# Side loads of x, first weights and gate combinations put behind other work in the instruction streams of a two-layer decoder kernel

## The chip, the core and the metric

The kernel runs on one core of one Trainium2 chip. The metric is the device time of one execution in microseconds; of the kernel before there are three timed runs and one profiled execution. The core has five engines with an instruction stream of their own: PE (TensorE, the matmuls), DVE (VectorE), ACT (ScalarE), POOL (GpSimd) and SP (SyncE), which here does nothing but issue DMA transfers. Each of the last four does its stream strictly in order, so an instruction that waits holds up everything behind it on that engine.

## The reference

The input x is 2048 tokens x 1024 features in float32. One chunked gMLP layer (layer A) is followed by one layer of dilated attention (layer B) that reads a shared key/value projection. Cut to what matters here:

```python
h = rms_norm(x, norm_g) * (1 + scale) + shift          # layer A
u, v, z = split(h @ w_in, 3)                           # 1024 -> 3 x 2048
v = rms_norm(gelu(v), sgu_g)
mixed = einsum('gts,bcsge->bctge', tril(w_s), chunks(v)) + b_s
x = x + gate * ((gelu(u) * mixed * silu(z)) @ w_out)   # 2048 -> 1024
k, v = split(ada(rms_norm(x)) @ w_kv, 2)               # shared, 6 kv heads of 128
q, z = ada(rms_norm(x)) @ w_in_b                       # 24 query heads, and 1024 of z
o = softmax-merge of three dilated attention groups
x = x + gate * ((o * silu(z)) @ w_out_b)
```

All projections are matrix products of 512 tokens with weight blocks; they fill most of the time of PE.

## The kernel before, in words

**Tiles and stages.** The tokens are taken in four quarters Q = 0 to 3 of 512 tokens (four tiles of 128). Quarter 0 runs layer A, then its share of layer B's projections (kv, q, z). Quarters 1 and 2 run layer A together in `layer_half`: first the v blocks (`dense_v`, names vh4 and vh5), then eight groups of u and z (`gate_block`, names uh0 to uh7 and zh0 to zh7), then each its output product and projections. Quarter 3 is like quarter 0, with its v blocks done by `dense_s2` (names v3). Attention for what is ready is woven in between as "fillers": Python generators that are advanced a step at a time by `tick` after every few matmuls.

**Precision.** Every product takes three matmul passes (`mm3`, L301): each operand is split into a high part and a low remainder, and high x high, low x high and high x low are summed. A weight block therefore takes this path: SP loads it raw (`raw_...`, 256 KB, L280, six buffers), ACT copies it to the high part (L272, about 0.63 us), DVE subtracts to get the low part (L273, about 0.69 us), and PE uses both (`w_...`, eight buffers). A weight unit that is late at any of the three is a stall of PE.

**Products.** Most blocks are done by Strassen-Winograd's 2x2 scheme with seven products. A product's name in a weight's name tells its weight block: 11, 12, 21, 22 are blocks as they are, t1 to t4 are combinations; `w_vh4t2_0` is the first unit of the t2 product of vh4. In the gates the combinations are made on the way, by DVE subtractions of loaded blocks (L744, `less`), since their tiles are small (128x512).

**Side work that the change touches.** `normed_T` prepares a later quarter's normalised and transposed input: it loads four tiles of x rows (`xa...`, 512 KB each, L864), squares them on ACT with a sum (L872), loads the transposed x (`xT...`, four pieces of 512 KB, L874), and makes the scale factors and products from both. It runs as a filler for quarter 1 (`xa00` to `xa03`, `xT1`), quarter 2 (`xa10` to `xa13`, `xT2`) and quarter 3 (`xa30` to `xa33`, `xT3`). `sums_A` loads quarter 3's stored input (`m3_1`) and makes sums of its parts (DVE, L1051 to L1054) and a split (`sA30`) that `dense_s2` uses from its fifth product on. `make_ops` makes split operands of layer B's input (`hob...`, L984 and L985). `product_out` adds the output product of layer A to the rows of x (`xr`, L1322), squares the sum on ACT (L1323), stores it (`x1d`, L1328), scales the rows (L1338), and PE transposes them (`pt_b`, L965, in `norm_T2`); in quarter 0 these transposes stand in the midst of the last output block's matmuls. `v_put` ends a v block's part with a gelu and a square on ACT (L1372, L1373), the latter over the PSUM tile itself.

**What sets the order.** The Tile framework's scheduler orders each engine's stream by its own cost model. `tc.issue_after(ins)` forces what is issued inside it to stand behind `ins`; it adds no wait across engines where the two are on one engine.

## Time and profile before

| | us |
|---|---|
| median of the three timed runs | 2913.62 |
| their lowest and highest | 2909.56, 2916.78 |
| time of the profiled execution | 2904.79 |
| span of its instructions | 2902.7 |
| PE busy in it | 2845.0 (98%) |
| DVE, ACT, POOL busy | 2199.5 (76%), 1629.5 (56%), 838.8 (29%) |
| DMA moved in it | 725.04 MB, mean 250 GB/s |
| mean granted clock of PE | 0.996 |

A busy PE here includes matmuls whose ends are modelled, so its 98% does not say that all of its time is at full speed. The time in which it stood still is told by the view of waits, and the time in which its clock was cut by the column PEclk of a view of time windows. The profile's lines carry the line numbers of the kernel; groups of tiles leave buffer numbers out, so `w_kv` stands for every weight unit of every kv block.

### The profile page before, as it was taken

The page shows a single profiled execution, that of the slowest core. Times are in us where ns is not written, and L with a number is a line of the kernel's source. Part 1 is how long each engine was busy: PE and PEld are TensorE (multiplying, and loading weights), DVE is VectorE, ACT ScalarE, POOL GpSimd, SP SyncE. Part 2 cuts the span into 40 slices and gives each one's busy share as a digit, 9 for nine tenths or more (in the row PEclk, how much of TensorE's full clock was granted, in tenths as well). Part 3 has the DMA queues.
Part 4 walks back from the last instruction along what each step waited for, and adds up shares of the span by engine and source line. Part 5 has one row for each costly group of instructions (what it writes and reads, how often), then busy time and mean ns, then how long its engine had stood idle before and what let it go on. Part 6 is the DMA issues. An engine that isn't in the chain of part 4 may idle for free.

```text
span 2902.7 us, 45106 instructions
## 1 busy us (share of the span) xinstructions
PE 2845.0 (98%) x14378; PEld 2381.9 (82%) x14378; DVE 2199.5 (76%) x4104; ACT 1629.5 (56%) x3302; POOL 838.8 (29%) x1097
## 2 busy tenths in 40 slices
PE   8999999999999999999999999999999999999999
PEld 5888878887888888878888788788888888888887
DVE  6877558787697789967787768789779676788682
ACT  4324346566556666545564656667666357876441
POOL 1067423440031025003315135115335121122322
PEclk9999999999999999999999999999999999999999
DMA  9899866888874655797989788855447867789653
GB/s 320 293 335 340 294 230 194 294 290 279 295 274 161 202 170 183 246 325 238 306 285 312 257 295 278 297 170 172 152 128 260 314 217 231 238 276 336 221 173 110
DMA packets 390449, 725.04 MB, mean 250 GB/s; under 512 B 42202, under 2 KB 119228, under 8 KB 389828
## 3 DMA queue, kind: packets, MB, share of 16 engines
q1 hardware_dynamic: 390212, 722.16, 74.3%
q8 instruction: 114, 1.87, 0.3%
q14 instruction: 123, 1.01, 0.1%
HBM read 547.81 MB, written 174.20 MB: 249 GB/s over the span
## 4 chain that ended last, share of the span: by engine, by line
PE 78%; DMA 8%; DVE 6%; issue 3%; ACT 3%; POOL 2%; SPq 0%; POOLq 0%; DVEq 0%; ACTq 0%
PE pd_kv L301 7%; PE po L1809 4%; PE pd_o L301 2%; PE pd_u L343 2%; PE pd_u L345 2%; PE pd_u L344 2%; PE pd_z L345 2%; PE pd_z L344 2%; PE pd_z L343 2%; PE pd_v L301 2%; PE pd_v3a L301 1%; PE pd_v3b L301 1%; PE pd_o3a L301 1%; PE pf L2002 1%; PE pf L2000 1%
## 5 line engine op out<-in xcount | busy, mean ns | idle before, releaser
L301 PE MATMUL pd_kv<-w_kv,hkh 128*128 128x512 f32 x672 | 209.3, 393 | 2.9 <-DVE w_kv L273 2.1
L1809 PEld LDWEIGHTS po<-kv,pT 128*128 128x128 f32 x1200 | 147.1, 191 | 15.7 <-POOL pT L1784 4.6
L1809 PE MATMUL po<-kv,pT 128*128 128x128 f32 x1200 | 150.6, 275 | 6.8 <-ACT pT L1655 2.8
L301 PEld LDWEIGHTS pd_kv<-w_kv,hkh 128*128 128x128 f32 x672 | 126.0, 189 | 30.7 <-DVE w_kv L273 3.2
L301 PE MATMUL pd_kv<-w_kv,hkl 128*128 128x512 f32 x336 | 131.0, 390 | 0.0
L272 ACT ACTIVATE w_q<-raw_q 128x512 fp32r<-128x512 f32 x144 | 89.1, 628 | 56.2 <-PE pd_kv L301 8.7
L1572 POOL TENSOR_SCALAR s_q<-s_q 128x4 f32<-128x4 f32 x96 | 24.2, 252 | 330.0 <-DVE s_q L1571 270.5
L1749 ACT ACTIVATE pr<-pr,stat,rt 128x256 f32<-128x256 f32 (+1 forms) x192 | 104.2, 545 | 25.8 <-DVE stat L1743 17.4
L1428 POOL TENSOR_SCALAR vc<-vc,rvh 128x256 f32<-128x256 f32 x64 | 65.4, 1041 | 183.7 <-DMA vc<-vh 132.5
L273 DVE TENSOR_TENSOR w_q<-raw_q,w_q 128x512 fp32r<-128x512 f32 x144 | 95.6, 685 | 22.2 <-ACT w_q L272 21.6
L2000 PE MATMUL pf<-wo,yb 128*128 128x512 f32 x256 | 104.5, 408 | 0.2 <-ACT yb L1963 0.2
L343 PE MATMUL pd_u<-hAh,w_u 128*128 128x512 f32 x256 | 103.5, 404 | 0.0
L343 PE MATMUL pd_z<-hAh,w_z 128*128 128x512 f32 x256 | 102.8, 401 | 0.0
L2002 PE MATMUL pf<-wo,yb 128*128 128x512 f32 x256 | 100.7, 394 | 0.0
L345 PE MATMUL pd_z<-hAh,w_z 128*128 128x512 f32 x256 | 100.3, 392 | 0.0
L345 PE MATMUL pd_u<-hAh,w_u 128*128 128x512 f32 x256 | 100.2, 391 | 0.0
L2001 PE MATMUL pf<-wo,yb 128*128 128x512 f32 x256 | 100.1, 391 | 0.0
L344 PE MATMUL pd_z<-hAl,w_z 128*128 128x512 f32 x256 | 99.9, 390 | 0.0
L344 PE MATMUL pd_u<-hAl,w_u 128*128 128x512 f32 x256 | 99.9, 390 | 0.0
L1749 ACT ACTIVATE st_pr<-st_pr,stat,rt 128x256 f32<-128x256 f32 (+1 forms) x128 | 73.5, 576 | 31.6 <-DVE stat L1746 18.2
L1757 POOL TENSOR_TENSOR dg<-pr,ident 128x256 f32<-128x256 f32 x38 | 31.2, 822 | 198.0 <-ACT pr L1749 132.6
L272 ACT ACTIVATE w_z<-raw_z 128x512 fp32r<-128x512 f32 x64 | 39.8, 628 | 81.8 <-PE pd_z L345 37.2
(1471 smaller groups left out, 8984.0 us busy)
## 6 DMA issues: line engine op xcount, KB each, us to landing
raw_q<-in_b_w_in_dram SPq DMA_DIRECT2D x144, 256.0 KB, 3.5
qt<-qd SPq DMA_DIRECT2D x96, 260.0 KB, 2.7
od<-ot SPq DMA_DIRECT2D x96, 256.0 KB, 3.0
w_o<-wtd SPq DMA_DIRECT2D x48, 512.0 KB, 5.2
raw_kv<-in_w_kv_dram SPq DMA_DIRECT2D x84, 256.0 KB, 4.1
kv<-kvd SPq DMA_DIRECT2D x75, 256.0 KB, 3.9
raw_u<-in_a_w_in_dram SPq DMA_DIRECT2D x64, 256.0 KB, 4.9
wt<-st_cw SPq DMA_DIRECT2D x64, 256.0 KB, 4.8
```

Source lines behind the costliest of these rows:

```text
L272: nc.scalar.activation(hi, src, AF.Copy)
L273: nc.vector.tensor_tensor(lo, src, hi.bitcast(F32), ALU.subtract)
L301: last_mm[0] = nc.tensor.matmul(pt, a, u[:, w, :], start=f, stop=e, skip_group_check=more)
L343: nc.tensor.matmul(pts[i], wh, hh[:, k, :], start=k == 0, stop=False)
L344: nc.tensor.matmul(pts[i], wh, hl[:, k, :], start=False, stop=False)
L345: nc.tensor.matmul(pts[i], wl, hh[:, k, :], start=False, stop=k == KT - 1)
L1428: nc.gpsimd.tensor_scalar(v[:, c, :], v[:, c, :], rvh[:, i:i + 1], None, ALU.mult)
L1749: nc.scalar.activation(pr[:, i, :], pr[:, i, :], AF.Exp, bias=mneg[:, i:i + 1], scale=u["rt"][:, h:h + 1], accum_out=lsum[:, i:i + 1])
L1809: nc.tensor.matmul(po[:, h * P:(h + 1) * P], u["pT"][h // hp][:, h % hp, j, :], u["kv"][:, j, kh, 1, :], start=j == 0, stop=j == nk - 1)
L2000: nc.tensor.matmul(pt, yb[:, 0, k, :], w_[:, 0, :], start=k == 0, stop=False)
L2001: nc.tensor.matmul(pt, yb[:, 0, k, :], w_[:, 1, :], start=False, stop=False)
L2002: nc.tensor.matmul(pt, yb[:, 1, k, :], w_[:, 0, :], start=False, stop=k == KT - 1)
```

## The change

Six edits of order; no instruction's work changes, and the only instructions that are added are three loads of activation tables on ACT, 93 in place of 90, that the new order brings with it.

1. `normed_T`: the loads of x rows and of xT are issued behind the last load of weights that the program has written so far (`last_ld`), and the squares behind the last high split of weights (`last_split[0]`).
2. `dense_v`: the splits of the product after "12/21" (the t2 product's) are issued behind the last square of the first half of that product's results.
3. `dense_o`: in its last product, the first weights of the kv projection are asked for ahead of the second half's matmuls.
4. `dense_s2`: the sums and the first split of `sums_A` are issued behind the low split of the t4 product's last weights.
5. `gate_block`: loading and combining a gate block's weights becomes a function of its own, `gate_raw`, called for the next block in the last product (t4) of the one before.
6. `make_ops`: the first puts ("11", "12") are issued behind the last splits of weights on ACT and DVE.

```diff
+    last_split = [None, None]
     def split(hi, lo, src):
-        nc.scalar.activation(hi, src, AF.Copy)
-        nc.vector.tensor_tensor(lo, src, hi.bitcast(F32), ALU.subtract)
+        last_split[0] = nc.scalar.activation(hi, src, AF.Copy)
+        last_split[1] = nc.vector.tensor_tensor(lo, src, hi.bitcast(F32), ALU.subtract)
...
-    def wunits(w, k0, n0, nm, nk=KT, ordered=False):
+    def wunits(w, k0, n0, nm, nk=KT, ordered=False, after=None):
...
-            split(u[:, 0, :], u[:, 1, :], raw)
+            with tc.issue_after(after.ins) if after else nullcontext():
+                split(u[:, 0, :], u[:, 1, :], raw)
...
                 if h:
                     store_late(0)
+                    if then is after:
+                        nxt.append(then())
...
-            nxt.append(then())
+            if then is not after:
+                nxt.append(then())
...
         ready = weights(b0, "t4")
-        late[0]()
+        with tc.issue_after(last_split[1].ins):
+            late[0]()
...
-    def gate_block(g, kind, ops, put, hooks={}):
+    def gate_raw(g, kind):
...
         raw["t3"] = raw["12"]
         less("t3", "22", "12")
+        return raw
+
+    def gate_block(g, kind, ops, put, raw, after, hooks={}):
...
             if w == "21":
                 raw["t4"] = raw["21"]
                 less("t4", "21", "t2")
+            if w == "t4":
+                raw.clear()
+                after()
             store_late(1)
...
         def c11(t, pt):
-            put(t, 0, pt, evt(f"{nm}a{t}"), pt)
+            return put(t, 0, pt, evt(f"{nm}a{t}"), pt)
...
+        half = []
         for a, q, first, take in (("11", "11", True, copy), ("12", "21", False, c11), ("s2", "t2", True, add_u),
...
-            us = wunits(*src[q], f"{nm}{q}_", 4)
+            us = wunits(*src[q], f"{nm}{q}_", 4, after=half.pop() if half else None)
...
                 for i in range(2):
-                    take(2 * pr + i, pts[i])
+                    done = take(2 * pr + i, pts[i])
+                if done and not pr:
+                    half.append(done)
...
             xts[t] = tile_of(t)
-            nc.sync.dma_start(xts[t], x[(Q * TPQ + t) * P:(Q * TPQ + t + 1) * P, :])
+            with tc.issue_after(last_ld[0].ins):
+                nc.sync.dma_start(xts[t], x[(Q * TPQ + t) * P:(Q * TPQ + t + 1) * P, :])
...
-            nc.scalar.activation(xts[t], xts[t], AF.Square, accum_out=sq[:, t:t + 1])
-        for k in range(0, KT, 2):
-            nc.sync.dma_start(xT[:, k:k + 2, :], x_t[k * P:(k + 2) * P, Q * QT:(Q + 1) * QT]
-                              .rearrange("(k p) t -> p k t", p=P))
+            with tc.issue_after(last_split[0].ins):
+                nc.scalar.activation(xts[t], xts[t], AF.Square, accum_out=sq[:, t:t + 1])
+        with tc.issue_after(last_ld[0].ins):
+            for k in range(0, KT, 2):
+                nc.sync.dma_start(xT[:, k:k + 2, :], x_t[k * P:(k + 2) * P, Q * QT:(Q + 1) * QT]
+                                  .rearrange("(k p) t -> p k t", p=P))
...
-            put("11", js, r0)
-            put("12", js, r1)
+            with tc.issue_after(last_split[0].ins), tc.issue_after(last_split[1].ins):
+                put("11", js, r0)
+                put("12", js, r1)
...
+        raws = {0: gate_raw(0, 0)}
         for g in range(8):
...
+            def prepare(i):
+                if i < 16:
+                    raws[i] = gate_raw(*divmod(i, 2))
+
-            gate_block(g, 0, ops, put_u)
-            gate_block(g, 1, ops, put_z, begin_y(got) if g == 7 else {})
+            gate_block(g, 0, ops, put_u, raws.pop(2 * g), lambda: prepare(2 * g + 1))
+            gate_block(g, 1, ops, put_z, raws.pop(2 * g + 1), lambda: prepare(2 * g + 2),
+                       begin_y(got) if g == 7 else {})
```

How this moves instructions is told by the streams themselves, at three places. The first is ACT at the end of quarter 0's output product. `w_o01_1_*` are the last output weights, `xa1*` rows of quarter 2's x, `w_kv02_*` the first weights of the kv projection, `xo0_1_*` the squares of the output rows on which the transposes `pt_b` depend. Before:

```order
L272 ACTIVATE w_o01_1_7_3472<-raw_o01_1_7_3473 128x512
L872 ACTIVATE xa11_4147,sqa2_4132<-xa11_4147 128x1024
L872 ACTIVATE xa12_4156,sqa2_4132<-xa12_4156 128x1024
L872 ACTIVATE xa13_4195,sqa2_4132<-xa13_4195 128x1024
L272 ACTIVATE w_kv02_0_0_3671<-raw_kv02_0_0_3672 128x512
L1323 ACTIVATE xo0_1_0_3531,sq10_0_2861<-xr0_0_2853 128x512
L1323 ACTIVATE xo0_1_1_3541,sq10_1_2862<-xr0_1_2854 128x512
```

After the change:

```order
L274 ACTIVATE w_o01_1_7_3472<-raw_o01_1_7_3473 128x512
L274 ACTIVATE w_kv02_0_0_3671<-raw_kv02_0_0_3672 128x512
L1349 ACTIVATE xo0_1_0_3531,sq10_0_2861<-xr0_0_2853 128x512
L1349 ACTIVATE xo0_1_1_3541,sq10_1_2862<-xr0_1_2854 128x512
L274 ACTIVATE w_kv02_0_1_3676<-raw_kv02_0_1_3677 128x512
```

The three squares of x rows are gone from here; they stand among the weights of the later block q02, and their loads and those of `xa00` with them have left SP's stream ahead of the store of the output rows. Likewise `xa00` to `xa03` move from block q02 to block q01, `xa30` to `xa33` from the kv blocks of quarter 2 to block q21, `xT2` from the start of the program to block q02, `xT1` and `xT3` behind the t4 loads of q01 and q21.

The second place is ACT at the turn from the product 12/21 to the product t2 of vh4. `pd_vh4a*` are PSUM tiles that the t2 product writes next; `ops*` are splits of another side work's sums (`fh*`). Before:

```order
L272 ACTIVATE ops3_6008<-fh511_6211 128x512
L272 ACTIVATE w_vh4t2_0_6236<-raw_vh4t2_0_6237 128x512
L272 ACTIVATE w_vh4t2_1_6241<-raw_vh4t2_1_6242 128x512
L272 ACTIVATE w_vh4t2_2_6246<-raw_vh4t2_2_6247 128x512
L1372 ACT_TABLE_LOAD
L1372 ACTIVATE vh4a0_6187<-pd_vh4a0_6022 128x512
L1372 ACTIVATE vh4a1_6190<-pd_vh4a1_6023 128x512
L1373 ACTIVATE pd_vh4a0_6022,sqh0_6010<-vh4a0_6187 128x512
L1373 ACTIVATE pd_vh4a1_6023,sqh0_6010<-vh4a1_6190 128x512
L272 ACTIVATE w_vh4t2_3_6251<-raw_vh4t2_3_6252 128x512
```

After the change:

```order
L274 ACTIVATE ops3_6008<-fh511_6211 128x512
L274 ACTIVATE ops4_6007<-fh512_6214 128x512
L1398 ACT_TABLE_LOAD
L1398 ACTIVATE vh4a0_6187<-pd_vh4a0_6022 128x512
L1398 ACTIVATE vh4a1_6190<-pd_vh4a1_6023 128x512
L1399 ACTIVATE pd_vh4a0_6022,sqh0_6010<-vh4a0_6187 128x512
L1399 ACTIVATE pd_vh4a1_6023,sqh0_6010<-vh4a1_6190 128x512
L274 ACTIVATE w_vh4t2_0_6236<-raw_vh4t2_0_6237 128x512
L274 ACTIVATE w_vh4t2_1_6241<-raw_vh4t2_1_6242 128x512
```

The t2 weights' high splits now stand behind the squares, and a split of another operand (`ops4` from `fh512`) stands ahead of the gelu. On DVE the low splits of `w_vh4t2_*` move in the same way behind three operations on `fh611` and `fh612`.

The third place is ACT at the start of gate block uh6, where attention's softmax (`stat1`, `kT0_3`) is woven in. `uh6t2` is a combination that DVE makes. Before:

```order
L1448 ACT_TABLE_LOAD
L1448 ACTIVATE pd_zh5t_9888<-pd_zh5t_9888 128x512
L774 ACTIVATE st_uh6u_10250<-pd_uh6x_10213 128x512
L1770 ACT_TABLE_LOAD
L1770 ACTIVATE stat1_195<-stat1_195 128x4
L1691 ACTIVATE kT0_3_10353<-pk0_3_10348 128x512
L1770 ACTIVATE stat1_195<-stat1_195 128x4
L272 ACTIVATE w_uh6t2_10253<-uh6t2_10209 128x512
L272 ACTIVATE w_uh6t1_10286<-uh6t1_10208 128x512
```

After the change:

```order
L1782 ACT_TABLE_LOAD
L1782 ACTIVATE pr0_2_01_10125,stat0_194<-pr0_2_01_10125,stat0_194,rt0_2_0_10016 128x256 x2
L1476 ACT_TABLE_LOAD
L1476 ACTIVATE pd_zh5t_9888<-pd_zh5t_9888 128x512
L793 ACTIVATE st_uh6u_10250<-pd_uh6x_10213 128x512
L274 ACTIVATE w_uh6t2_10253<-uh6t2_10160 128x512
L274 ACTIVATE w_uh6t1_10286<-uh6t1_10159 128x512
L274 ACTIVATE w_uh621_10339<-raw_uh621_10157 128x512
L1724 ACTIVATE kT0_3_10353<-pk0_3_10348 128x512
```

The split of the t2 combination stands directly behind the copy of the first product, the table load and the softmax pieces behind it; one more change of table stands shortly ahead.

More of the change, by code (lines that the diff above doesn't have):

```diff
@@ L1 @@
-from contextlib import ExitStack
+from contextlib import ExitStack, nullcontext
 from itertools import chain
@@ L749, in gate_block, with less @@
         less("t3", "22", "12")
+        return raw
+    def gate_block(g, kind, ops, put, raw, after, hooks={}):
+        nm = f"{'uz'[kind]}h{g}"
+        def less(o, a, b):
+            nc.vector.tensor_tensor(raw[o], raw[a], raw[b], ALU.subtract)
         def product(pt, a, w, first):
@@ L1372, in v_put @@
         nc.scalar.activation(dst, src, AF.Gelu_apprx_tanh)
-        nc.scalar.activation(junk, dst, AF.Square, accum_out=sqh[t // 4][:, t % 4, j:j + 1])
+        last = nc.scalar.activation(junk, dst, AF.Square, accum_out=sqh[t // 4][:, t % 4, j:j + 1])
         stores.append([0, lambda: nc.sync.dma_start(vh[t * P:(t + 1) * P, j * 512:(j + 1) * 512], dst)])
+        return last
     def in_long():
```

## The prediction

> **What bounds the kernel now.** The page gives PE 2845.0 of 2902.7 us, so I read first the waits of PE, to see which of its stops the six edits touch. Columns: engine, line, what it waited for, total us, times, longest.
>
> ```profile
> PE pt_b L965 <- DVE xr L1338: 5.1, 1, 5.1
> PE pd_vh4a L301 <- ACT pd_vh4a L1373: 4.3, 2, 3.6
> PE pd_uh6y L762 <- ACT w_uh6t L272: 2.7, 1, 2.7
> PE pd_v3a L301 <- ACT w_v L272: 2.3, 1, 2.3
> PE pd_kv L301 <- DVE w_kv L273: 2.1, 2, 1.1
> PE pd_zh3y L762 <- ACT w_zh3t L272: 1.7, 1, 1.7
> PE pd_v3a L301 <- DVE w_v L273: 0.9, 1, 0.9
> PE pd_zh5y L762 <- ACT w_zh5t L272: 0.9, 1, 0.9
> PE pd_uh6y L762 <- DVE w_uh6t L273: 0.3, 1, 0.3
> ```
>
> Together 20.3 us, at places where something that the edits move stands ahead of what PE needs. Second I read windows behind the long ones (stretch, its length, PE busy (matmuls), granted clock, DMA share, GB/s).
>
> ```profile
> 406.00:412.70 6.70, 4.88 (x15) 0.50 0.76 273
> 665.30:668.70 3.40, 3.40 (x10) 0.50 0.91 269
> 1102.20:1105.60 3.40, 3.08 (x8) 0.50 0.00 0
> 1849.70:1853.10 3.40, 3.40 (x10) 0.51 0.97 350
> ```
>
> After each of the four longest stops PE runs at half clock for a while. What it does there would take half the time at full clock, so the cuts cost 4.88/2 = 2.4, then 1.7, 1.5 and 1.7 us more. The most that the edits could win is 20.3 + 7.3 = 27.6 us, 1% of the span.
>
> **A rule on the clock.** [...] The rows show it halved after stops of 2.7 + 0.3 and of 2.3 + 0.9 us too. [...]
>
> **Quarter 0's output product (edit 1).** PE waits for the scaled rows of the output. What they wait for stands in the timelines (start, us, operation, idle before it and what ended it).
>
> ```profile
> 395.32 1.06 ACT L872 ACTIVATE xa<-xa 128x1024 f32<-128x1024 f32 x1 [3.70 <-DMA xa<-in_x_dram]
> 400.02 1.06 ACT L872 ACTIVATE xa<-xa 128x1024 f32<-128x1024 f32 x1 [3.54 <-DMA xa<-in_x_dram]
> 401.60 0.62 ACT L1323 ACTIVATE xo<-xr 128x512 f32<-128x512 f32 x1
> 396.52 1.29 DVE L1322 TENSOR_TENSOR xr<-xr,xo 128x512 f32<-128x512 f32 x2
> 406.92 0.76 DVE L1338 TENSOR_SCALAR xr<-xr,r_b 128x1024 f32<-128x1024 f32 x1 [2.16 <-DMA x1d<-xr]
> 396.50 5.02 SPq L864 DMA_DIRECT2D xa<-in_x_dram  x2
> 401.62 0.86 SPq L1328 DMA_DIRECT2D x1d<-xr  x2
> 407.82 1.09 PE L965 MATMUL pt_b<-ident,xr 128*128 128x128 f32 x4 [5.14 <-DVE xr L1338]
> ```
>
> The two row tiles are summed by 397.2 and 397.8, but their squares begin at 401.6, behind squares of x rows that wait 3.7 and 3.5 us for their loads. The store is late as well: SP sits from 396.50 on loads of x rows whose buffers those squares free, and issues it at 401.62. The scaling, which overwrites the rows, waits for the store until 406.92. With the x rows off both engines, squares and store begin at about 397.8, 3.8 us earlier. From 401.62 to 406.92 took 5.3 us, so the scaling comes at 403.1 and PE at 404.0 in place of 407.8. Its stop is then 5.1 − 3.8 = 1.3, shorter than any that was followed by a cut: 5.1 + 2.4 − 1.3 = 6.2. If the store no longer holds the scaling up (2.16), the stop is gone: 7.5. If the transposes, which now stand up to 8 matmuls earlier in PE's stream, give that shift back as a wait (8 x 0.23 = 1.8), it is 4.4. I take **+6.2**, range 4 to 7.5.
>
> **vh4 (edit 2).** PE waits here for the squares of the first half's results. Taken by itself the edit promises the whole stop, 3.6 + 1.7.
>
> ```profile
> 658.02 0.69 DVE L926 TENSOR_TENSOR fh<-fh 128x512 f32<-128x512 f32 x1
> 661.63 1.28 ACT L1372 ACT_TABLE_LOAD   x1
> 662.92 1.08 ACT L1372 ACTIVATE vh4a<-pd_vh4a 128x512 f32<-128x512 f32 x2
> 665.06 0.69 DVE L926 TENSOR_TENSOR fh<-fh,fh 128x512 f32<-128x512 f32 x1
> 664.67 7.36 PE L301 MATMUL pd_vh4a<-w_vh4t,ops 128*128 128x512 f32 x24 [3.57 <-ACT pd_vh4a L1373]
> ```
>
> But in the new stream the split of `fh512` stands ahead of the table load. DVE's first operation on it is the row of 658.02; with the low split of `fh511` and the second operation, 0.7 us each, it is ready at about 660.0. Its high split ends at 660.6, the table load at 661.9, one us earlier than now, the squares at about 664.0, and the first t2 weight's high split, now behind them, at 664.6: PE could start when it does now. The low split of that weight stands on DVE behind the row of 665.06 and ends at 666.4, while PE asks for it two matmuls in, at 665.1. That is 1.3 us lost. Behind it on DVE wait the three other low splits, 0.7 each, faster than PE uses them. I take **−1.3**. The bounds are +5.3, if the loads of `fh` come early enough to clear both engines, and −2.6, if another operation of 1.3 gets in. vh5's t2 splits are treated alike: table load 1.3, gelu 1.1, squares 1.2, first split 0.7 + 0.7 make 5.0 us from the end of a half product, and the other half keeps PE busy for 24 matmuls, 7.36 − 1.7 = 5.7 at full clock: 0, and a stop of under 1 if one more operation gets in.
>
> **Gates (edit 5).** The start of uh6:
>
> ```profile
> 1097.36 1.28 ACT L1770 ACT_TABLE_LOAD   x1
> 1098.30 1.09 DVE L744 TENSOR_TENSOR uh6t<-raw_uh,raw_uh 128x512 f32<-128x512 f32 x1 [0.66 <-DMA raw_uh<-in_w_uz_dram]
> 1100.41 1.15 ACT L272 ACTIVATE w_uh6t<-uh6t 128x512 fp32r<-128x512 f32 x2 [0.97 <-DVE uh6t L744]
> ```
>
> ACT splits at 1100.41 because DVE combined from 1098.3 to 1100.3, and that because the load had just landed. Begun a product earlier (12 matmuls, 2.7 us, and the attention pieces between) the combination is there in time. The stops of uh6 (2.7 + 0.3 and 1.5 of clock), zh3 (1.7) and zh5 (0.9) make 7.1. Against it stand three table loads more, 3 x 1.28 = 3.8 us of ACT. With none of them on PE's path the gain is 7.1, with all of them 3.3; I take the middle, **+5.2**, since some stand ahead of a gelu whose PSUM tile PE writes next and some do not. The range goes down to 0, if such a gelu comes late twice.
>
> [...]
>
> **kv weights (edits 3 and 6).** The kv stops are low splits that stand behind four low puts of `hob`:
>
> ```profile
> 1277.30 2.49 DVE L985 TENSOR_TENSOR hob<-st_b,hob 128x512 fp32r<-128x512 f32 x4
> 1280.31 0.68 DVE L273 TENSOR_TENSOR w_kv<-raw_kv,w_kv 128x512 fp32r<-128x512 f32 x1
> ```
>
> The puts go behind kv weights, and nothing reads them before the q products that follow the kv blocks. 2.49 is more than the longest stop, 1.1. **+2.0**, range 1 to 2.1. Edit 3 leaves SP's stream here as it was: 0.
>
> **v3 (edit 4).**
>
> ```profile
> 1843.24 1.23 DVE L1053 TENSOR_TENSOR m<-m 128x1024 f32<-128x1024 f32 x1
> 1846.50 2.17 ACT L272 ACTIVATE w_v<-raw_v 128x512 fp32r<-128x512 f32 x4
> 1838.67 2.35 SPq L280 DMA_DIRECT2D raw_v<-in_a_w_in_dram  x4
> raw_v<-in_a_w_in_dram SPq DMA_DIRECT2D x48, 256.0 KB, 4.2
> 1843.78 1.07 PE L301 MATMUL pd_z2bb<-w_z2b,hob 128*128 128x512 f32 x4
> ```
>
> The first weight lands at 1838.7 + 4.2 = 1842.9. With no sums and no `sA` ahead of them its two splits end at 1842.9 + 0.6 + 0.7 = 1844.2, before PE is free at 1844.85; now they begin at 1846.50. Stop and cut go, 2.3 + 0.9 + 1.7 = 4.9; I keep 0.4 for a later unit: **+4.5**, range 2 to 4.9. The sums, four of 1.23, then share DVE with the splits of the third product; they are first read by the fifth.
>
> **Moved loads (edit 1).** Each of three quarters puts 2 MB of x rows (four loads) among weights, and quarter 2's xT (four more) goes into q02:
>
> ```profile
> 450.00:500.00 50.00, 49.79 (x224) 41.08 (x223) 36.13 (x63) 32.88 (x62) 18.29 (x33) 1.00 0.63 191
> 500.00:550.00 50.00, 50.00 (x222) 41.23 (x221) 36.31 (x58) 24.47 (x41) 19.35 (x33) 1.00 0.90 295
> 1700.00:1750.00 50.00, 49.72 (x220) 40.86 (x219) 35.57 (x57) 28.97 (x50) 18.74 (x36) 1.00 0.91 308
> xT<-in_x_t_dram SPq DMA_DIRECT2D x12, 512.0 KB, 6.8
> ```
>
> 2 MB at 300 GB/s are 7 us of DMA. In the first window a share of 0.63 leaves 18 us for 14; in the others 0.9 leaves 5 us, so 2 us lie over. Against them stands the weights' lead: of eight buffers a product holds four, so the next product's four are made during 24 matmuls, 5.7 us. I take **−1**, range −6 (the 2 us twice and a cut) to 0. What xT2's leaving the start brings I put at 0.
>
> **Sum.** 6.2 − 1.3 + 5.2 + 2.0 + 4.5 − 1.0 = 15.6. For an execution like the profiled one 2904.8 − 15.6 = 2889.2; that one lies 8.8 below the median of the timed runs, where 2913.6 − 15.6 = **2898**.
>
> **Rivals.** *All of it* (0.08): vh4 goes too and nothing new comes, 27.6, so 2886. Every row of the first fence is for it, the new stream of vh4 against it. *Waits only change place* (0.20): the table loads eat the gates (0), quarter 0 gives 4.4, kv and v3 the lower ends (1 + 2), vh4 −1.3, the moved loads −5: a gain of 1, 2912.5. For it speaks that at vh4 and v3 the next piece is ready only within a us of need; against it, that five places would have to turn out badly at once. *The x rows bring their waits along* (0.11) is the slower side. On ACT an x square waits for its load, and every weight split behind it with it: 3.7 and 3.5 us in the rows of 395 and 400. Twelve squares now stand among the splits of blocks q02, q01 and q21. If each waits w, a block loses 4w beyond the lead of about 6 us. At 3.6 that is 8 a block, 24 in all, and a cut of 1.7 in each: 29 against the 16.6 won elsewhere, 2913.6 + 12.5 = 2926. It makes the kernel slower from w = 2.5 on ((10 − 6) x 3 + 5 = 17). Against it: in those rows the loads waited for buffers that the squares themselves held, and each load now follows directly behind a weight's load, its square behind that weight's split, so w should be the 1.7 us that 512 KB take at 300 GB/s. [...] That the change moves nothing is excluded by the streams.
>
> **Numbers.** The forecast, a gain of 9 to 20, has 0.61. 0.3%, about what a measurement of this kernel can tell, is 8.7 us. Faster: 0.61 + 0.08 and a little of the second case, 0.70; the same: 0.19; slower: the third, 0.11. The single bounds add up to gains from −1.6 to 27, which is 2915 to 2887; the range is 2886 to 2914 and leaves out the slow case. The forecast's own is 2890 to 2905.
>
> **What would show it.** Right: no square of x rows between 385 and 405, a stop before `pt_b` of under 2 us and no half clock behind it; no stop of a gate over 1 us; v3's first splits done as PE comes free. vh4 keeps a stop of 3 to 5 us that now ends with a low split on DVE. Wrong: ACT waiting for `xa` over 1.5 us a time in q02, q01 or q21 and PE stopping behind it, or a new stop of a gate behind a table load.

## The result, and the profile after the change

| | before | after |
|---|---|---|
| median of the timed runs, us | 2912.5 | 2906.8 |
| lowest and highest, us | 2908.6, 2920.1 | 2899.2, 2913.6 |
| ratio with its 95% interval | | 0.9978 [0.9968, 0.9987] |
| time of the profiled execution, us | 2904.8 | 2902.7 |

The change gains 6.4 us, between 3.8 and 9.3, where 15.6 were forecast. The sign was right and 2906.8 lies in the range of 2886 to 2914, but it is outside the forecast's own 2890 to 2905, and 0.22% is less than the 0.3% that was called a difference. Gains in microseconds are from here on (1 − ratio) times the kernel before's median.

The profiled execution of before was a quick one, below each of the 22 timed runs in this table, so the two profiles differ by only 2.1 us. The total cannot be compared in them, and single stops vary from one execution to the next (the last section says by how much).

First the waits of PE in the kernel after. Columns as in the prediction: engine, line, what it waited for, total us, times, longest.

```profile
PE pd_vh4a L304 <- ACT w_vh4t L274: 5.5, 1, 5.5
PE pk L1719 <- DVE ot L1848: 3.9, 1, 3.9
PE pr_a L913 <- POOL on L908: 3.1, 1, 3.1
PE pd_zh5y L781 <- ACT w_zh5t L274: 1.7, 1, 1.7
PE pd_v3a L304 <- DVE w_v34t L275: 0.8, 1, 0.8
PE pd_v3a L304 <- DVE w_v L275: 0.5, 2, 0.3
PE pt_b L990 <- DVE xr L1364: 0.5, 1, 0.5
PE pd_kv L304 <- DVE w_kv L275: 0.5, 2, 0.3
```

Of the five largest stops in the prediction's list, `pt_b` fell from 5.1 to 0.5, v3's first weights from 2.3 + 0.9 to 0.7, and the kv weights from 2.1 to 0.5. The stop of 2.7 at uh6's second product (`pd_uh6y`) is gone by name, but a new one of 3.9 (`pk`) stands directly ahead of that product. `pr_a` is new too, and vh4's stop is longer. Next, stretches of time (start and end, length, then busy us and instructions of PE, PEld, DVE, ACT, POOL, then granted clock, DMA share, GB/s). The kernel before:

```profile
400.00:450.00 50.00, 44.03 (x199) 35.88 (x197) 40.96 (x73) 33.28 (x68) 5.29 (x8) 0.93 0.58 188
1840.00:1860.00 20.00, 16.77 (x66) 13.13 (x65) 17.45 (x23) 13.21 (x22) 0.00 (x0) 0.91 0.85 285
```

The kernel after, with the cuts of its clock behind the stops at vh4 and at the gates:

```profile
400.00:450.00 50.00, 49.50 (x234) 40.75 (x234) 43.74 (x77) 34.49 (x70) 5.09 (x9) 1.00 0.56 177
1840.00:1860.00 20.00, 19.54 (x84) 15.30 (x82) 14.43 (x19) 13.40 (x24) 0.00 (x0) 1.00 0.89 300
659.30:666.10 6.80, 5.64 (x12) 4.09 (x13) 5.97 (x10) 6.31 (x15) 0.00 (x0) 0.50 0.96 283
1096.20:1103.00 6.80, 4.97 (x14) 3.80 (x15) 6.80 (x17) 3.76 (x6) 6.64 (x8) 0.50 0.34 117
```

At the end of quarter 0's output product and at v3, PE is now busy for 49.50 of 50 and 19.54 of 20 us, at full clock (1.00). Behind vh4's and the gate's stops the half clock lasts 6.8 us where it lasted 3.4. A cut of 3.4 us at 1601 (granted clock 0.50), behind a stop of 2.9 in attention (`po`), is new, and one at 2410 was there before, at 2413. Up to the last microseconds of the program both profiles spend 20.5 us at half clock.

To weigh stages I took the distance of each matmul's start to the next, less the usual (median) distance for its shape, and summed this loss over a stage:

| stage, us of the span | what it holds | lost before | lost after |
|---|---|---|---|
| 400 to 450 | end of quarter 0's output product | 9.0 | 0.9 |
| 450 to 640 | blocks with the moved loads | 0.4 | 3.3 |
| 640 to 720 | vh4 | 6.8 | 8.7 |
| 790 to 1205 | gates | 13.8 | 17.2 |
| 1205 to 1300 | kv | 4.7 | 2.9 |
| 1840 to 1950 | v3 | 5.4 | 3.1 |
| all of the span | | 99.6 | 97.1 |

**The new stop at `pr_a`.** These matmuls spread quarter 2's scale factors; POOL makes their diagonals `rd`. They stand in PE's stream behind the first weight of q02's product t1, before and after alike. The timelines of POOL and PE after (start, us, operation, idle before it and what ended it):

```profile
473.08 0.19 POOL L1605 TENSOR_SCALAR s_q<-s_q 128x4 f32<-128x4 f32 x1 [9.51 <-DVE s_q L1604]
479.58 0.20 POOL L908 MEMSET on<- 128x128 f32 x1
469.81 5.60 PE L304 MATMUL pd_q02b<-w_q02t,hob 128*128 128x512 f32 x24
479.83 1.16 PE L913 MATMUL pr_a<-rd,on 128*128 128x128 f32 x8 [3.06 <-POOL on L908]
```

And before:

```profile
480.60 0.19 POOL L1572 TENSOR_SCALAR s_q<-s_q 128x4 f32<-128x4 f32 x1 [13.98 <-DVE s_q L1571]
485.94 0.20 POOL L883 MEMSET on<- 128x128 f32 x1
479.01 5.60 PE L301 MATMUL pd_q02b<-w_q02t,hob 128*128 128x512 f32 x24
486.19 1.16 PE L888 MATMUL pr_a<-rd,on 128*128 128x128 f32 x8 [0.21 <-POOL on L883]
```

Counted from the start of the product t3 (the row of `pd_q02b`), POOL gets `s_q` 3.3 us in (473.08 − 469.81) where it got it 1.6 in, 1.7 later, and then takes 6.7 us to the end of the memset where it took 5.5 (the four diagonals alone took 4.3 for 3.1). That is the 2.9 us that the stop has grown by. The scale factors themselves had been ready since 463.57, so the squares of x are not late; the diagonals only stand behind `s_q` in POOL's stream. Why `s_q` comes later is told by a wait of ACT in this window after the change:

```profile
ACT w_q02t L274 <- DMA raw_q02t<-wt: 4.3, 2, 4.1
```

Here stand the moved loads: SP issues the four pieces of xT2 from 452.8 to 458.9 and the weights of t3 behind them, so ACT sits 4.1 us until 466.29 for the first of these. PE still gets its weights in time, but ACT's work on the queries (`hs_q`, from which `s_q` comes) stands behind seven weight splits and begins 1.8 us into the product (471.63) where it began 0.15 into it.

**vh4.** ACT and PE after:

```profile
655.54 0.63 ACT L274 ACTIVATE ops<-fh 128x512 fp32r<-128x512 f32 x1 [2.12 <-DVE fh L951]
656.19 1.28 ACT L1398 ACT_TABLE_LOAD   x1
659.68 2.18 ACT L274 ACTIVATE w_vh4t<-raw_vh4t 128x512 fp32r<-128x512 f32 x4
660.36 8.01 PE L304 MATMUL pd_vh4a<-w_vh4t,ops 128*128 128x512 f32 x21 [5.54 <-ACT w_vh4t L274]
```

As predicted, a split of `fh` now stands ahead of the table load and the first t2 weight is split only behind the squares: PE starts 0.05 us after the end of that weight's high split (659.68 + 0.63). ACT waits 2.12 us for the `fh` sum, and the table load begins at 656.19, when PE has already stood still for 1.4 us (its stop began at 660.36 − 5.54 = 654.82).

**Gates.** SP, PE and DVE around uh6 after:

```profile
1086.47 0.89 SPq L743 DMA_DIRECT2D raw_uh<-in_w_uz_dram  x1
1086.60 0.62 PE L781 MATMUL pd_uh6x<-op,w_uh 128*128 128x512 f32 x2
1094.00 1.23 DVE L751 TENSOR_TENSOR uh6t<-raw_uh,raw_uh 128x512 f32<-128x512 f32 x1 [2.59 <-DMA raw_uh<-in_w_uz_dram]
1097.38 0.59 DVE L1848 SCALAR_TENSOR_TENSOR ot<-o,stat,po 128x128 f32<-128x128 f32 x2
1098.03 1.11 PE L1719 MATMUL pk<-ident,kv 128*128 128x128 f32 x4 [3.86 <-DVE ot L1848]
```

And before:

```profile
1091.39 0.62 PE L762 MATMUL pd_uh6x<-op,w_uh 128*128 128x512 f32 x2
1093.17 0.42 SPq L736 DMA_DIRECT2D raw_uh<-in_w_uz_dram  x1
```

PE reaches uh6 4.8 us earlier than before (1086.60 for 1091.39), so times are counted from there. The load that the combination waits for is issued 0.1 us ahead of that start, where it was issued 1.8 us behind it. Yet the first combination begins 7.4 us into the block (1094.00), where it began 6.9 us in (1098.30): no earlier at all. DVE stands idle for the load for 2.6 us, and attention's `ot`, which follows in DVE's stream, keeps PE waiting for 3.9. The t2 combination itself is done 10.3 us in (8.9 before), so uh6 would have waited without `pk` as well.

### The profile page after: what moved, and what is told of

It is laid out like the page before. It is cut to its first block, busy times and chain, and to the rows that moved or that the text cites. A ratio compares the mean times of both kernels' runs of the same rounds, so it can differ in the third digit from the quotient of the medians.

```text
span 2900.7 us, 45101 instructions
## 1 busy us (share of the span) xinstructions
PE 2844.0 (98%) x14378; PEld 2382.0 (82%) x14378; DVE 2203.0 (76%) x4104; ACT 1632.6 (56%) x3305; POOL 844.8 (29%) x1097
## 4 chain that ended last, share of the span: by engine, by line
PE 78%; DVE 6%; DMA 6%; issue 4%; ACT 3%; POOL 2%; SPq 0%; POOLq 0%; DVEq 0%; ACTq 0%
PE pd_kv L304 7%; PE po L1842 4%; PE pd_o L304 3%; PE pd_v L304 2%; PE pd_u L346 2%; PE pd_u L348 2%; PE pd_u L347 2%; PE pd_z L348 2%; PE pd_z L346 2%; PE pd_z L347 2%; DMA qt<-qd 2%; PE pd_o1a L304 1%; PE pf L2035 1%; PE pf L2033 1%; PE pf L2034 1%
## 5 line engine op out<-in xcount | busy, mean ns | idle before, releaser
L1782 ACT ACTIVATE pr<-pr,stat,rt 128x256 f32<-128x256 f32 (+1 forms) x192 | 104.3, 545 | 26.5 <-DVE stat L1776 17.2
```

What stands on the lines that cost most here:

```text
L1782: nc.scalar.activation(pr[:, i, :], pr[:, i, :], AF.Exp, bias=mneg[:, i:i + 1], scale=u["rt"][:, h:h + 1], accum_out=lsum[:, i:i + 1])
```

## The experiments

Each kernel ran in 5 to 12 timed runs beside 12 to 35 of the kernel before. With 12 runs the interval of a gain is about ±3.5 us.

**1. Edit 1 alone.** The loads and squares of x; the other five edits are out.

```diff
+            with tc.issue_after(last_ld[0].ins):
+                nc.sync.dma_start(xts[t], x[(Q * TPQ + t) * P:(Q * TPQ + t + 1) * P, :])
...
+            with tc.issue_after(last_split[0].ins):
+                nc.scalar.activation(xts[t], xts[t], AF.Square, accum_out=sq[:, t:t + 1])
```

> The kernel before with edit 1 alone (loads and squares of x rows, loads of xT). Theory from the changed kernel's trace: quarter 0's stop before the transposes and its half clock go (excess of PE's time in the stage 400 to 450 from 9.0 to about 1 us), and a new stop of about 3 us comes at about 480, where PE waits for POOL's diagonals of quarter 2's row scales (the matmul pr_a), since the squares that feed them now come late. Net 5 us faster, 2907 against 2912. Rival (the slower case of the prediction): the loads of x among the weights make ACT wait for x rows over 1.5 us a time and PE stop for weights in the blocks q02, q01 and q21; then 2912 or more. Rival: the edit also pays in the start, where quarter 2's xT has left the queue; then the first 100 us are shorter by more than 1 us.

Ratio 0.9980 [0.9968, 0.9991], a gain of 5.8 [2.6, 9.3]. The waits of PE between 440 and 720 us:

```profile
PE pd_vh4a L304 <- ACT pd_vh4a L1394: 4.3, 2, 3.8
PE pr_a L909 <- POOL on L904: 2.6, 1, 2.6
```

The stage from 400 to 450 loses 1.1 in place of 9.0, the one from 450 to 640 loses 6.5 in place of 0.4: the stop at `pr_a`, 3.4 us of half clock behind it and a stop of 1.0. So the edit wins 7.9 and, in this execution, gives 6.1 back; in the whole change's profile, where no cut followed the stop at `pr_a` (granted clock 1.00 from 478 to 494), it was 2.9. The theory above blamed late squares of x for that stop; `r_a`, which is made from them, is ready at 464.1 here, 9.4 us before POOL gets `s_q` and goes on. In none of the three quarters does ACT wait for an x row, so the slower rival's w is 0 here.

**2. Edit 5 alone.** The gates' combinations a product earlier.

```diff
+            gate_block(g, 0, ops, put_u, raws.pop(2 * g), lambda: prepare(2 * g + 1))
+            gate_block(g, 1, ops, put_z, raws.pop(2 * g + 1), lambda: prepare(2 * g + 2),
```

> The kernel before with edit 5 alone (the next gate block's loads and combinations asked for in the last product of the block before). Theory from the changed kernel's trace: the combination now stands earlier in DVE's stream but its load lands hardly earlier, so DVE waits at it and holds up attention's pieces behind it, for which PE waits; the stops of the gate stage (13.7 us in all from 790 to 1205 before) grow to 15 to 17: 2912 + 3 = 2915. Rival (the prediction): the stops of uh6, zh3 and zh5 go and 5 us are won, 2907; the longer stops seen in the changed kernel would then come from other edits. Rival: stops only change place, 2912.

Ratio 0.9997 [0.9985, 1.0009], a gain of 0.9 [−2.6, 4.4]. The waits of PE in the gates (950 to 1205 us):

```profile
PE pk L1711 <- DVE ot L1840: 1.5, 1, 1.5
PE pd_zh5y L777 <- ACT w_zh5t L274: 1.4, 1, 1.4
PE pd_uh6y L777 <- DVE w_uh6t L275: 0.9, 1, 0.9
```

The stop at zh3 is gone, as promised, but that at zh5 has grown (0.9 before), and at uh6 one of 1.5 stands at `pk` beside one of 0.9. The stage loses 13.6 us. In seven profiles with the gates' order of the kernel before (with those of experiments 9, 13 and 14 below) it loses 13.8 to 19.1; so the 17.2 of the whole change does not show that the gates became slower.

**3. Edits 4 and 6 alone.** The sums ahead of v3, and the first puts of `hob`.

```diff
+        with tc.issue_after(last_split[1].ins):
+            late[0]()
...
+            with tc.issue_after(last_split[0].ins), tc.issue_after(last_split[1].ins):
+                put("11", js, r0)
+                put("12", js, r1)
```

> The kernel before with edits 4 and 6 (quarter 3's sums behind the t4 weights' low split; first puts of layer B's operands behind the last splits). Theory: the stop of 2.5 + 1.2 us and the half clock at v3 go (excess in 1840 to 1860 from 5.4 to 1 us), about 2 us come back in the next 90 us, where the sums now stand among the splits of the third product; the kv stops at 1281 and 2304 shrink from 1.2 to 0.4 each. Net 4 to 5 us, 2908. Rival: the sums cost where they go what they cost where they were, and nothing is won, 2912.

Ratio 0.9992 [0.9980, 1.0004], a gain of 2.3 [−1.2, 5.8]. v3's waits of PE:

```profile
PE pd_v3a L304 <- DVE w_v34t L275: 0.8, 1, 0.8
PE pd_v3a L304 <- DVE w_v L275: 0.8, 2, 0.6
PE pd_v3a L304 <- ACT w_v L274: 0.8, 1, 0.8
```

3.2 us became 2.4, a third of it new: the moved sums now stand ahead of the splits of `w_v34t`. kv's two stops fell from 2.1 to 0.5. Over all profiles the stage of v3 loses 2.7 us on average in the six that have the two edits (1.5 to 3.9) and 5.8 in the seven with the order of the kernel before there (3.5 to 8.8), so its gain is nearer to 3 than to the 0.8 of the waits alone. In the other three (experiments 9, 10 and 14) the order at v3 shifted without these edits.

**4. Edit 2 alone.** The t2 splits of vh4 and vh5 behind the squares.

```diff
+            us = wunits(*src[q], f"{nm}{q}_", 4, after=half.pop() if half else None)
```

> The kernel before with edit 2 alone (splits of vh4's and vh5's t2 weights behind the squares of the product 12/21). Theory: the table load of the gelu waits on ACT for the split of a side sum (fh512), and the low splits wait on DVE behind further side sums, so the stop at the turn to t2 grows from 3.7 to about 6 us, with up to twice the time at half clock (3.4 to 6.8 us at half): 2 to 4 us slower, 2915. Rival (the prediction's size): 1.3 us lost and no more, 2913. Rival (the edit as it reads): the squares come earlier and the stop of 3.7 us and its half clock go, 2907.

Ratio 1.0006 [0.9993, 1.0018], a loss of 1.7, between 5.2 lost and 2.0 won. The wait of PE is about as long as before, and what ends it is now the weight's high split:

```profile
PE pd_vh4a L304 <- ACT w_vh4t L274: 4.0, 1, 4.0
```

The low split behind it cost 0.3 more. The four parts sum to 5.8 + 0.9 + 2.3 − 1.7 = 7.3, and the whole gains 6.4: with intervals this wide no disturbance of one edit by another can be seen. Edit 3 was not run alone.

**5 and 6. Do the gates hang on the combination or on its load?** Of a gate's four blocks, 12 lies in a pool of buffers that it shares with side work, and its load is the last of the four on SP, behind transfers of attention. Here that pool goes to block 21, which is needed later; none of the six edits is in the first kernel, edit 5 is in the second.

```diff
-            pool, tag = (ep, "ev") if i == 1 else (rp, "raw")
+            pool, tag = (ep, "ev") if i == 2 else (rp, "raw")
```

> The kernel before, none of the six edits; only the two pools of a gate block's tiles are exchanged: the block 12, from which every combination is made, takes a buffer of the pool of raw weights, and the block 21, needed last, the one of the shared pool that comes free late. So the load of 12 stands with those of 11 and 22 in SP's stream. Theory: what the stops of uh6 and its like wait for is that one late load, whatever the place of the combination; then the stop of 2.2 to 3.9 us at uh6 falls under 0.5 and the gate stage (790 to 1205), 13.8 to 16.6 us of excess in the three profiles in which the gates are untouched, to 10 or less: 2908 against 2912. Rival: the place of the combination in DVE's and ACT's streams decides, and a stop of 2 us or more stays at uh6.

> The same exchange of pools with edit 5 on top. Theory: with the loads there in time the early combination no longer holds DVE up; PE's stop before pk (1.5 to 3.9 us with edit 5 alone) goes, and the edit pays what it promised at zh3 and zh5 as well: 2906, 1 to 2 us below the exchange alone. Rival: asking for combinations early holds up attention's pieces on DVE by itself; then a stop behind DVE stays and the time is that of the exchange alone or more.

Ratios 0.9985 [0.9973, 0.9998] and 0.9981 [0.9971, 0.9990], gains of 4.4 [0.6, 7.9] and 5.5 [2.9, 8.4]. With the exchange alone, this is the longest wait left at a gate block:

```profile
PE pd_uh7x L777 <- DVE w_uh L275: 0.7, 1, 0.7
```

uh6, zh3 and zh5 no longer wait. But the exchange alone also moves the combinations. With it, and without edit 5, the first combination of uh6 stands among the work of zh5:

```profile
1080.69 0.68 DVE L747 TENSOR_TENSOR uh6t<-raw_uh,raw_uh 128x512 f32<-128x512 f32 x1
1089.55 0.62 PE L777 MATMUL pd_uh6x<-op,w_uh 128*128 128x512 f32 x2
```

That is 8.9 us ahead of uh6's first matmul, where it came 6.9 us behind it; at zh3 and zh5 it likewise moves 16 to 18 us ahead. So this run does not separate the load from the place of the combination. That the load holds uh6 and zh5 up is shown by the runs with edit 5 and without the exchange: there DVE is idle at these combinations until the load lands (2.6 and 1.7 us in the whole change, 0.7 and 1.0 with edit 5 alone). At zh3 it was not the load: in the kernel before, its combinations were done 4.2 us before PE came to need them, and ACT's split stood behind attention's work; edit 5 alone removes that stop. Edit 5 on top of the exchange takes the stage's loss from 11.0 to 7.0 in the profiles, and its stop at `pk` does not come, but in the timed runs the two differ by less than their intervals.

**7 and 8. Both repairs.** Edits 1, 2, 4 and 6, with two mends, and then with the exchange. The first mend puts `pr_a` two steps of the filler later. The second clears vh4: the side sums on `fh` go mostly into product 11 and stop in product 21, and from the fifth on they stand behind the last weights' splits.

```diff
         nc.gpsimd.memset(one_, 1.0)
         yield
+        yield
+        yield
         yield
         pr = pst(f"pr_a{Q}")
...
-                    tick(0.25)
+                    tick({"11": 0.4, "21": 0.0}.get(q, 0.25) if b == 4 else 0.25)
...
+            if i > 3:
+                for e in last_w:
+                    behind.enter_context(tc.issue_after(e.ins))
```

> Edits 1, 2, 4 and 6 (edit 5 left out) with two mends. In the preparation of a quarter's x two steps are put ahead of the matmul pr_a, so that it stands 18 matmuls later in PE's stream; and at vh4 four steps of the side sums are run in the product 11 and none in 12/21, while the later ones are issued behind the last weights' splits, so that neither ACT nor DVE has a side sum ahead of the squares and the t2 splits. Theory: the stop of 2.7 to 3.2 us at pr_a goes, the stop at vh4 falls from 4 to 6 us to under 1 with no half clock behind it, and with quarter 0's and v3's gains the kernel takes 2896 (5.8 + 2.9 + 5 + 2.3 under 2912). Rival: what is won at vh4 comes back where the side sums now pile up (products 11 and t2 to t1), 2901. Rival: the pr_a stop is not one of place but of work on POOL and stays.

> The kernel fixed with the exchange of pools for the gate blocks. Theory: the gains lie in different stages and add up, 4 us below fixed: 2892. Rival: they do not add up, since PE arrives earlier at what is late anyway; then as fixed.

Medians 2889.6 and **2888.2**, ratios 0.9919 [0.9903, 0.9936] and 0.9914 [0.9900, 0.9928]: 23.6 and 25.0 us faster than before, and some 18 faster than the change. The exchange adds nothing that can be measured here, though the gates lose 11.0 us in its profile and 16.8 without it. PE's wait at vh4, with the exchange and then without:

```profile
PE pd_vh4a L305 <- ACT w_vh L274: 4.5, 1, 4.5
```

```profile
PE pd_vh4a L305 <- ACT w_vh L274: 1.1, 1, 1.1
```

In both, ACT waits here (4.2 and 3.9 us) for weights whose loads stand behind those of the side sums drawn into product 11. The longer stop cannot be the exchange's doing: up to 765 us the two kernels have the same order on every engine. It is a difference between two executions, and where the exchange's gain in the gates goes stays open.

**9 and 10. What is each mend worth?** Edit 1 with the first mend, and edit 2 with the second.

```diff
+        yield
+        yield
         yield
         pr = pst(f"pr_a{Q}")
```

> Edit 1 alone with its mend: the matmul pr_a two steps later in PE's stream. Edit 1 alone took 5.8 us off and had a stop of 2.7 us and 3.4 us of half clock (1.7 us) at pr_a. Theory: the mend takes that stop and cut, 4 us, so 9 to 10 us under the kernel before: 2902. Rival: the stop moves with the matmul, or the scale that is late holds up the next work (quarter 2's h), 2906.

> Edit 2 alone with its mend (side sums behind the splits of the t2 weights, four steps of them pulled into the product 11). Edit 2 alone moved the time by nothing that shows (+1.3 us). Theory: the stop at the turn to t2 (3.7 to 4.1 us and 3.4 us at half clock) goes, and a new one of 1 to 5 us comes ahead of the product 12/21, whose weights land late behind the loads of the pulled side sums: 1 to 4 us under the kernel before, 2909. Rival: no stop is left, 2906. Rival: the new stop takes all of it, 2912.

Ratios 0.9942 [0.9926, 0.9959] and 0.9961 [0.9941, 0.9980], gains of 16.9 [11.9, 21.6] and 11.4 [5.8, 17.2]. The second is better than expected: vh4 loses 1.4 us (6.6 with edit 2 alone, 4.0 to 9.3 in seven profiles with the order of the kernel before), and this is left of the wait:

```profile
PE pd_vh4a L305 <- ACT w_vh L274: 0.6, 1, 0.6
```

The order at v3 also shifted in it, by no edit of its own; that stage loses 2.5. The first mend is worth 11 us more than edit 1 alone, too much for a stop of 2.6 and its cut. Its profile shows the stops at vh4 (2.4 in place of 4.3) and at v3 (3.5 in place of 5.6) shorter as well, though nothing there was edited. So a second theory was due: the steps of quarter 1 or 3, also put later, do that.

**11 and 12. A gentler second mend.** The side sums' steps spread over product 11 and half of 21, without and with edit 5.

```diff
-                    tick({"11": 0.4, "21": 0.0}.get(q, 0.25) if b == 4 else 0.25)
+                    tick(0.25 if b != 4 or q not in ("11", "21") else 0.3 if q == "11" or not pr else 0.0)
```

> As fixed_swap, but with fewer side sums pulled ahead at vh4 (three steps in the product 11, the fourth in the first half of 12/21), so that the loads of the weights of 12/21 stand ahead of the fifth step's loads in SP's stream. Theory: the stop of 1.2 to 4.6 us for those weights goes (their data landed 4 us late behind the side sums' loads), and the stop at the turn to t2 stays under 1.5: 2884, 4 us under fixed_swap. Rival: what the weights of 12/21 wait for are free buffers, not the loads ahead, and the stop stays: 2888.

> fixed2 with edit 5 on top, that is all the edits but the one without effect, and three mends and the exchange of pools. Theory: with the loads in time edit 5 is worth 0 to 2 us, 2883. Rival: early combinations hold up attention's pieces on DVE, 2886 or more.

Ratios 0.9923 [0.9906, 0.9940] and 0.9919 [0.9902, 0.9936]. The wait for the weights of product 12/21 at vh4 falls to 0.2 in the first of them, yet the times are those of the two kernels above. The theory took the 4.5 of one execution for the rule; the two other kernels with the sums drawn into product 11 waited 1.1 and 0.6, so there was little to win. Edit 5 is worth nothing measurable here either, though the gates lose 8.6 with it and 12.3 without.

**13 and 14. Which quarter's steps?** Edit 1 with the first mend in quarter 2 alone, and in quarters 1 and 3 alone.

```diff
+        if Q == 2:
+            yield
+            yield
```

> Edit 1 alone, with the two steps ahead of pr_a in quarter 2's preparation only (13 rows of PE's stream stand elsewhere than in edit 1 alone). Theory: the whole gain of the mend (11 us between the two medians) belongs to the stop of 2.7 us at quarter 2's pr_a, its half clock and what follows in the same stage, so this kernel takes 2896 to 2902. Rival: the gain came from quarters 1 and 3, whose preparations the mend also set two steps later; then 2907 as edit 1 alone.

> Edit 1 alone, with the two steps in the preparations of quarters 1 and 3 only; quarter 2's pr_a stays where edit 1 left it. Theory: the stop at pr_a stays (2.7 to 3.2 us) and the time is that of edit 1 alone, 2907. Rival: 2896 to 2902, since the later places of quarter 1's and 3's loads, sums and products free DMA or DVE for weights (its stops at vh4 and v3 would then be shorter than the 4.0 and 5.6 us of edit 1 alone).

Ratios 0.9975 [0.9962, 0.9988] and 0.9961 [0.9945, 0.9977], gains of 7.3 [3.5, 11.1] and 11.3 [6.7, 16.0]. The first has no stop at `pr_a` and gains 1.5 over edit 1 alone, less than the two can be told apart by. The second keeps that stop (2.7) and gains 5.5 more, which is about what the two can be told apart by, again with a shorter wait at vh4:

```profile
PE pr_a L912 <- POOL on L904: 2.7, 1, 2.7
PE pd_vh4a L304 <- ACT pd_vh4a L1397: 2.2, 1, 2.2
```

ACT ahead of vh4's gelu there:

```profile
654.30 0.63 ACT L274 ACTIVATE w_vh4t<-raw_vh4t 128x512 fp32r<-128x512 f32 x1 [0.28 <-DMA raw_vh4t<-wt]
654.95 1.28 ACT L1396 ACT_TABLE_LOAD   x1
```

And with edit 1 alone:

```profile
657.34 0.63 ACT L274 ACTIVATE w_vh4t<-raw_vh4t 128x512 fp32r<-128x512 f32 x1 [0.59 <-DMA raw_vh4t<-wt]
658.13 1.27 ACT L274 ACTIVATE w_vh4t<-raw_vh4t 128x512 fp32r<-128x512 f32 x2 [0.15 <-DMA raw_vh4t<-wt]
659.42 1.28 ACT L1393 ACT_TABLE_LOAD   x1
```

One t2 split stands ahead of the table load instead of three, which take 1.9 us and wait 0.7 for their loads. The order at v3 shifted as well: of the two splits of sums that stood ahead of the first weights on ACT, one now stands between them. In the two kernels with the later steps of quarters 1 and 3 the stages of vh4 and v3 lose 3.7 and 2.3 us, and 3.2 and 2.3; in the two without, 7.8 and 8.8, and 9.3 and 3.5. So the theory that the whole gain is that of `pr_a` is not borne out, and accidental orders at vh4 and v3 are the likely rest; how much each is worth is not shown. The two parts, 1.5 and 5.5, fall 4 short of the 11 of both together, which is well inside the uncertainty of such a sum (some ±8).

## Why the prediction was right or wrong

| term | predicted | measured |
|---|---|---|
| quarter 0 and the moved loads (edit 1) | 6.2 − 1.0 = 5.2 | 5.8 [2.6, 9.3] |
| vh4 (edit 2) | −1.3 | −1.7 [−5.2, 2.0] |
| gates (edit 5) | 5.2 | 0.9 [−2.6, 4.4] |
| kv and v3 (edits 3, 4, 6) | 2.0 + 4.5 = 6.5 | 2.3 [−1.2, 5.8] (4 and 6) |
| sum | 15.6 | 6.4 [3.8, 9.3] |

**Quarter 0: right in total, by two errors.** The chain from the x rows to the late squares, the store and the scaling was read rightly; the scaling comes in time and the stop is gone with its cut, so the upper bound of 7.5 was the better value (8 in the stage). Of the moved loads the working asked whether PE's weights would come late, and set their lead of 5.7 us against 7 us of DMA. That lead held for PE. It did not hold for what stands behind the splits on ACT: the queries' work, 1.7 us late, and through DVE and POOL the diagonals of `pr_a`. So the term of −1 was too small: stage 450 to 640 lost 2.9 more in the whole change and 6.1 more with edit 1 alone. That the two errors cancel to the measured 5.8 is luck.

**vh4: right in kind, its size not to be told.** That edit 2 would not free PE, because a split of `fh` stands ahead of the table load and the weights come behind the squares, is what all rows show. But the wait was to end with a low split on DVE, 1.3 us late; it ends with the high split on ACT, and the low split cost 0.3 with edit 2 alone. In the whole change the table load, reckoned to begin 0.5 us before PE stops, began 1.4 us after, since ACT waited for the `fh` sum. With an unedited order PE's waits at vh4 measured 2.9 to 5.7 us in seven profiles, so neither the 4.0 nor the 5.5 tells −1.3 from nothing. The kernel with the second mend bears out the bound on the other side, "if the loads of `fh` come early enough": with the sums out of the way the stage loses 1.4.

**Gates: the step that failed** is "Begun a product earlier … the combination is there in time". The row that it rested on said that DVE's combination had waited 0.66 us "because the load had just landed", and the working moved the combination without asking what moves the load. At uh6 the load was issued 1.9 us earlier in PE's terms and took longer: DVE's start came 7.5 us after its issue, where it came 5.1 after. So the combination began no earlier, DVE waited 2.6 us in place of 0.66, and attention was held up. At zh5 the load was issued no earlier at all (0.5 us ahead of the block, 0.9 before), and PE's stop grew from 0.9 to 1.7. The working also put zh3 under the same cause; its combinations had been done in time, the stop was one of ACT's order, and there the edit paid its 1.7. Of the 5.2 the timed runs show 0.9, at most 4.4. The three table loads, on which the range was built, show up in no wait of PE.

**kv: right** (2.1 to 0.5, predicted 2.0, measured 1.6 in the waits). **v3: mis-sized, the second step that failed.** The mechanism holds, but 4.5 was taken from one stop and its cut of one execution; the stage gained 2.3 between the two profiles and some 3 on average, and the timed runs give 2.3 for kv and v3 together, of the 6.5 predicted. The working said that the moved sums "share DVE with the splits of the third product" and gave that no price; they cost 0.8 at `w_v34t`, and the first splits still came up to 0.8 late.

**Cuts of the clock.** That each goes with its stop was my estimate, 7.3 us in all, of which the sum counted those of quarter 0, the gates and v3 (up to 5.6). Two went, at quarter 0 and v3. The two at vh4 and the gates became twice as long, 1.7 us more each, and one came behind a stop in attention that had had none, so between these two profiles the clock won nothing (20.5 us at half clock in each).

**The rivals.** The nearest was "waits only change place", which had 0.20 and priced the gates at 0 and v3 and kv at 3, both as measured. It went too far in asking that five places turn out badly; two did. That was enough, so what I held against it was no evidence. The slower side did not come: the x squares wait for nothing on ACT, less than the 1.7 us that the working allowed them.

## What to carry to other kernels

An operation that was moved earlier gained nothing where its load was not: it then waited in the stream and held up the next one (at uh6 DVE waited 2.6 us for the load, and PE 3.9 for the `ot` behind it), so ask first which pool or queue sets the time of the load. Where loads were put among weights, the weights' own lead covered the matmuls, but not the work that stands behind the weights' splits on the same engine (in q02 ACT waited 4.1 us for a weight, `hs_q` came 1.7 later, and PE stopped for 3.1 at `pr_a`); follow that to whoever waits for it. And the stop at the turn of two products was shortened more by what stands ahead of it (side sums, splits that wait for loads) than by moving the waiting pieces themselves: vh4's stage lost 1.4 us with the second mend and 6.6 with edit 2 alone.

## What the runs showed of the hardware

**The length of a stop alone did not tell whether a half clock came with it.** In the kernel before, the granted clock was 0.50 for 6.8 us with the stop of 5.1 at `pt_b`, and for 3.4 with those of 3.6 at vh4, 2.7 + 0.3 at uh6 and 2.3 + 0.9 at v3; in the kernel after, for 6.8 with the stops of 5.5 at vh4 and 3.9 at `pk`, and for 3.4 with that of 2.9 at `po`. It began between 1.9 us ahead of a stop's end and 1.4 behind it. The clock stayed at 1.00 with the stop of 3.1 at `pr_a` after, and with one of 2.3 at `po` before. The same stop in the same code, `pr_a` with 2.6 and 2.7 us, went both ways. First the kernel with edit 1 alone, then the one with the mend in quarters 1 and 3, each in two stretches of 3.4 us:

```profile
477.49:480.90 3.41, 1.05 (x9) 1.05 (x10) 1.77 (x3) 0.46 (x1) 3.24 (x7) 1.00 0.81 252
480.90:484.32 3.42, 3.42 (x10) 2.65 (x10) 2.64 (x5) 1.23 (x2) 0.69 (x3) 0.50 0.26 97
```

```profile
475.78:479.19 3.41, 2.34 (x11) 1.61 (x9) 3.41 (x7) 2.14 (x4) 3.41 (x7) 1.00 0.80 259
479.19:482.61 3.42, 1.82 (x12) 1.71 (x13) 1.01 (x2) 0.60 (x1) 3.09 (x6) 1.00 0.80 250
```

In the first, the stop of 2.6 us lies almost whole in one stretch, with PE busy for 1.05 us of it, and the next stretch ran at 0.50; in the second, the stop of 2.7 us is shared by both, with PE busy for 2.34 and 1.82 us, and the clock was 1.00 in each. What decides is not shown.

**One execution is a small sample.** In seven profiles in which every engine has the same order at v3, its first stop on ACT measured from 1.6 to 5.0 us, and the stages of vh4 and of the gates lost 4.0 to 9.3 and 13.8 to 19.1 in seven profiles each with the same order. The timed runs of the kernel before lie between 2903.2 and 2924.3 in all. A term that is read from one profile, as the 4.9 of v3, carries that spread.
